# Five forms of the product that reads the middle rows of a two-layer decoder trunk

## The chip, the cores and the metric

The kernel runs on one core of a Trainium2 chip. The metric is the device time of one execution in microseconds (us), as the median over several executions; lower is better. One execution was also recorded by the hardware profiler, and all rows shown below come from such recordings.

## The reference

Two layers over a sequence of 256 tokens with 2048 features, all in float32. Layer 0 mixes tokens by retention with 8 heads, layer 1 by a short gated convolution of width 3. Each mixer is followed by a SwiGLU feed-forward block with 5632 inner features. Each sub-layer is fed by an RMS norm with a scale and shift that come from the conditioning vector `c`, and is added back with a gate.

```python
for i in range(DEPTH):
    mod = (c_act @ w_mod[i] + b_mod[i])[:, None, :]
    sh1, sc1, g1, sh2, sc2, g2 = jnp.split(mod, 6, axis=-1)
    h = (rms_norm(x, norm1_g[i]) * (1.0 + sc1) + sh1).astype(x.dtype)
    ...          # i = 0: y = retention_mixer(h, ...); i = 1: y = short_conv_mixer(h, ...)
    x = (x + g1 * y).astype(x.dtype)
    h = (rms_norm(x, norm2_g[i]) * (1.0 + sc2) + sh2).astype(x.dtype)
    x = (x + g2 * swiglu(h, ffn_w_in[i], ffn_w_out[i])).astype(x.dtype)
return rms_norm(x, final_g).astype(x.dtype)

def swiglu(h, w_in, w_out):
    a, b = jnp.split(h @ w_in, 2, axis=-1)
    return (jax.nn.silu(a) * b) @ w_out
```

## The kernel before

Features lie on the 128 partitions and the 256 tokens along the free dimension, so an activation of 2048 features is 16 rows of 128x256. Every float32 value is kept as a sum of two parts, a high one and a low one. A row therefore holds 2 x 256 numbers: the 256 tokens' high parts and then their low parts. A weight block of 128x128 is split in the same way into `hi` and `lo`. A product of a block with a row needs three partial products: `hi` with the row's high part, `hi` with its low part, and `lo` with its high part.

`product` (line 345) makes them with two matmuls for each block: `hi` against all 512 numbers of the row (line 355), which fills both halves of a PSUM bank, and `lo` against the 256 high parts (line 358), added to the second half. I call these two matmuls a *unit*. `packed` (line 365) makes the same three partial products with three matmuls of 256 columns (lines 378 to 380) that are all added into one half of a bank. It is used for the queries, keys and gates of the retention, and for the last column of an output. `values` (line 794) holds the activation as the stationary operand and streams 512 columns of weights in each of its three matmuls (lines 801 to 803).

A `Group` is a list of output columns (128 features each) and of rows `ks`. `product` walks over the rows and, for each row, over the columns. Weights come in one long stream in just this order of use: `laid_out` writes them so, `prepare` (line 295) takes 1 MB from memory, and for each half of it (8 units) ScalarE makes the `hi` part (line 310) and VectorE the `lo` part (line 313). `take` keeps two such halves prepared ahead. TensorE's instructions are issued in the order of the program text. The order on the other engines is chosen by the compiler's scheduler from priorities.

Five stages read *middle rows*, the tiles `mid`:

| stage | what | rows | units with 512 columns | packed units |
|---|---|---|---|---|
| 0 | layer 0, feed-forward, first half of the inner features | 22 | 352 | 0 |
| 1 | layer 0, feed-forward, second half | 22 | 330 | 22 |
| 2 | layer 1, output of the convolution | 16 | 240 | 16 |
| 3 | layer 1, feed-forward, first half | 22 | 352 | 0 |
| 4 | layer 1, feed-forward, second half | 22 | 330 | 22 |

Each is an `output` (line 517) over 16 columns. Its first group takes two columns together (four in stage 2) and all but the last two rows (the last one in stage 2), so that the stage can begin before the last middle rows are written. Then each of these columns gets its remaining rows, and the other columns follow one at a time. After a column, two VectorE instructions add it to the residual `x[j]` (lines 535 and 536). In the second half of a feed-forward block, and in stage 2, squares for the next norm follow, and `scaled_only` (line 461) writes the next stage's row `h[j]`. The last column of those stages is `packed`. Between the columns `paced` (line 267) lets through the modulation steps (line 244), each of them 1 MB from memory and one VectorE instruction over 128x2048.

Before the change each middle row is a tile of its own, 22 tiles of 2 KB on each partition. The rows `h` that the other stages read are slices of one tile, `h_all`, in which one row is 2 x 258 numbers long (line 458).

Of the kernel before, what the change touches and what calls it, by code (L numbers as in the profile page):

```python
# [49 lines left out]
RAW_BUFS = 3  # L50
PART_BUFS = 4
# [49 lines left out]

def halves(rows):
    n = rows // P // 2
    return [range(n), range(n, 2 * n)]
# [25 lines left out]
FFN_OUT = out_groups(halves(DFF), 2, LEAD_FFN)  # L130


def in_use_order():
# [10 lines left out]
    for layer in range(DEPTH):  # L144
        if layer == 1:
            for g in CONV_IN:
                yield "conv_w_in", 0, g
            for g in CONV_OUT:
                yield "conv_w_out", 0, g
        for part in range(2):  # L150
            for g in FFN_IN[part]:
                yield "ffn_w_in", layer, g
            for g in FFN_OUT[part]:
                yield "ffn_w_out", layer, g
# [31 lines left out]
def trunk(ctx: ExitStack, tc: tile.TileContext, x_in, c_in, pos_in, w_mod, cols_in, tab_in, w_all, out):  # L186
# [158 lines left out]
    def product(g, act, base=0, before=None, banks=None, last=True):  # L345

        fresh = not banks
        banks = banks or [bank() for _ in g.cols]
        for k in g.ks:
            if before:  # L350
                before(k)
            h = act[k - base]
            for c, pt in zip(g.cols, banks):
                hi, lo = take(g, k, c)
                nc.tensor.matmul(  # L355
                    pt, hi, h, start=fresh and k == g.ks[0], stop=False, skip_group_check=True
                )
                nc.tensor.matmul(  # L358
                    pt[:, 1, :], lo, h[:, 0, :], start=False, stop=last and k == g.ks[-1], skip_group_check=True
                )  # L360
            ticked(len(g.cols))
        paced(len(g.cols) * len(g.ks))
        return banks
# [153 lines left out]
    def output(groups, act, which, last, after=None, base=None):  # L517
# [5 lines left out]
        for j, g in enumerate(groups):  # L523
# [9 lines left out]
            (pt,) = product(g, act, base, banks=banks[j : j + 1])  # L533
# [378 lines left out]
    mpool = ctx.enter_context(tc.tile_pool(name="mpool", bufs=1))  # L912

# [4 lines left out]
    def swiglu(layer, acc, after):  # L918
        n = FT // 2
        for part, groups in enumerate(FFN_IN):  # L920
            mid = [mpool.tile([P, 2, S], F32R, tag=f"mid{i}", name=name("mid")) for i in range(n)]
# [14 lines left out]
            acc = output(FFN_OUT[part], mid, (layer, GT2), part == 1, after if part else None)  # L936
# [5 lines left out]
    mid = [mpool.tile([P, 2, S], F32R, tag=f"mid{i}", name=name("mid")) for i in range(KT)]  # L942
# [82 lines left out]
```

## Time and profile before

| | us |
|---|---|
| median of three runs | 2654.03 |
| lowest, highest run | 2652.48, 2657.95 |
| span of the profiled execution | 2658.0 |

The span, from the first to the last instruction of the profiled execution, is as long as the highest of the runs, so there is nothing to add around it. It is 4.0 us (0.15%) above the median.

How to read the rows: PE is TensorE with its matmuls, PEld are its weight loads, which overlap the matmuls. DVE is VectorE, ACT is ScalarE, SP the queue that issues loads. In a row of a group of instructions stand line, engine, operation, output and inputs, shapes, count, busy time, mean nanoseconds of one, and then the idle time of the engine before them with what ended it. The duration of a matmul has a modelled end and overlaps the next one. What counts is the distance from one start to the next.

### The profile page before, as it was taken

The page shows a single profiled execution, that of the slowest core. Times are in us where ns is not written, and L with a number is a line of the kernel's source. Part 1 is how long each engine was busy: PE and PEld are TensorE (multiplying, and loading weights), DVE is VectorE, ACT ScalarE, POOL GpSimd, SP SyncE. Part 2 cuts the span into 40 slices and gives each one's busy share as a digit, 9 for nine tenths or more (in the row PEclk, how much of TensorE's full clock was granted, in tenths as well). Part 3 has the DMA queues.
Part 4 walks back from the last instruction along what each step waited for, and adds up shares of the span by engine and source line. Part 5 has one row for each costly group of instructions (what it writes and reads, how often), then busy time and mean ns, then how long its engine had stood idle before and what let it go on. Part 6 is the DMA issues. An engine that isn't in the chain of part 4 may idle for free.

```text
span 2658.0 us, 40105 instructions
## 1 busy us (share of the span) xinstructions
PE 2622.0 (99%) x16044; PEld 2340.2 (88%) x16044; DVE 2019.7 (76%) x2646; ACT 1260.0 (47%) x1819; POOL 153.5 (6%) x230
## 2 busy tenths in 40 slices
PE   7999999999999999999999999999999999999998
PEld 6998889889989888888888898888998888888887
DVE  7888988787698877777777889878887665555554
ACT  5545543444456444344444454444554443444443
POOL 0000000120000010100000001100000000000000
PEclk9999999999999999999999999999999999999999
DMA  9975668777676876777777758776776755444453
GB/s 397 396 274 220 224 232 315 263 269 280 239 271 252 319 282 262 300 269 280 283 278 276 273 219 321 289 276 258 265 269 256 264 220 190 184 187 189 190 190 127
DMA packets 96958, 687.70 MB, mean 259 GB/s; under 512 B 10753, under 2 KB 12545, under 8 KB 13825
## 3 DMA queue, kind: packets, MB, share of 16 engines
q1 hardware_dynamic: 96194, 684.48, 67.6%
q8 instruction: 125, 2.05, 0.3%
q10 hardware_dynamic: 576, 0.66, 0.1%
q14 instruction: 63, 0.52, 0.1%
HBM read 682.99 MB, written 2.10 MB: 258 GB/s over the span
## 4 chain that ended last, share of the span: by engine, by line
PE 75%; issue 19%; DVE 3%; DMA 1%; ACT 0%; POOL 0%; SPq 0%; POOLq 0%; ACTq 0%; DVEq 0%
PE bank L355 35%; PE bank L358 18%; PE bank L380 4%; PE bank L378 4%; PE bank L379 4%; PE bank L802 2%; PE bank L803 2%; PE bank L801 2%; PE bank L494 1%; PE bank L493 1%; PE bank L495 1%; DMA raw<-w_all 1%; DMA raw<-w_mod 1%; DVE lo L313 1%; DVE raw L619 0%
## 5 line engine op out<-in xcount | busy, mean ns | idle before, releaser
L313 DVE TENSOR_TENSOR lo<-raw,hi 128x1024 fp32r<-128x1024 f32 x912 | 1112.6, 1224 | 550.1 <-ACT hi L310 548.1
L310 ACT CAST hi<-raw 128x1024 fp32r<-128x1024 f32 x912 | 953.6, 1050 | 1101.8 <-PE bank L355 632.4
L355 PE MATMUL bank<-h,hi 128*128 128x512 f32 x3296 | 1155.2, 395 | 0.0
L358 PE MATMUL bank<-h,lo 128*128 128x256 f32 x3296 | 926.2, 281 | 0.0
L355 PEld LDWEIGHTS bank<-h,hi 128*128 128x128 f32 x3296 | 623.0, 189 | 144.1
L358 PEld LDWEIGHTS bank<-h,lo 128*128 128x128 f32 x3296 | 623.3, 189 | 0.0
L355 PE MATMUL bank<-mid,hi 128*128 128x512 f32 x1604 | 557.4, 394 | 0.0
L358 PE MATMUL bank<-mid,lo 128*128 128x256 f32 x1604 | 446.0, 278 | 0.0
L244 DVE SCALAR_TENSOR_TENSOR raw<-raw,cb 128x2048 f32<-128x2048 f32 x160 | 365.7, 2286 | 12.5 <-DMA raw<-w_mod 12.0
L355 PEld LDWEIGHTS bank<-mid,hi 128*128 128x128 f32 x1604 | 301.2, 188 | 70.2
L358 PEld LDWEIGHTS bank<-mid,lo 128*128 128x128 f32 x1604 | 301.5, 188 | 0.0
L380 PE MATMUL bank<-h,lo 128*128 128x256 f32 x1024 | 292.0, 285 | 6.2 <-DVE lo L313 6.2
L378 PE MATMUL bank<-h,hi 128*128 128x256 f32 x1024 | 291.9, 285 | 3.5 <-ACT h L644 3.5
L379 PE MATMUL bank<-h,hi 128*128 128x256 f32 x1024 | 291.3, 284 | 0.0
L380 PEld LDWEIGHTS bank<-h,lo 128*128 128x128 f32 x1024 | 195.7, 191 | 7.1 <-DVE lo L313 7.1
L378 PEld LDWEIGHTS bank<-h,hi 128*128 128x128 f32 x1024 | 197.3, 193 | 3.9 <-ACT h L644 3.8
L379 PEld LDWEIGHTS bank<-h,hi 128*128 128x128 f32 x1024 | 195.9, 191 | 0.2 <-DVE h L645 0.2
L355 PE MATMUL bank<-rm,hi 128*128 128x512 f32 x496 | 175.9, 399 | 0.1
L358 PE MATMUL bank<-rm,lo 128*128 128x256 f32 x496 | 139.5, 281 | 0.0
L355 PEld LDWEIGHTS bank<-rm,hi 128*128 128x128 f32 x496 | 93.3, 188 | 22.7 <-DVE rm L395 0.4
L802 PE MATMUL bank<-lo,h 128*128 128x512 f32 x256 | 101.8, 398 | 4.2 <-DVE lo L313 4.2
L801 PE MATMUL bank<-hi,h 128*128 128x512 f32 x256 | 102.2, 399 | 0.0
(155 smaller groups left out, 2190.2 us busy)
## 6 DMA issues: line engine op xcount, KB each, us to landing
raw<-w_all SPq DMA_DIRECT2D x456, 1024.0 KB, 4.9
raw<-w_mod SPq DMA_DIRECT2D x192, 1024.0 KB, 5.1
x<-x_in SPq DMA_DIRECT2D x4, 512.0 KB, 5.7
decay<-tab_in SPq DMA_DIRECT2D x8, 128.0 KB, 3.7
out<-out SPq DMA_DIRECT2D x4, 256.0 KB, 3.1
out<-out ACTq DMA_DIRECT2D x3, 128.0 KB, 2.7
out<-out SPq DMA_DIRECT2D x1, 384.0 KB, 2.6
out<-out ACTq DMA_DIRECT2D x1, 256.0 KB, 3.2
```

Source lines behind the costliest of these rows:

```text
L244: nc.vector.scalar_tensor_tensor(raw, raw, 1.0, cb, op0=ALU.mult, op1=ALU.mult, accum_out=total)
L310: nc.scalar.copy(hi, raw)
L313: nc.vector.tensor_tensor(lo, raw, hi.bitcast(F32), op=ALU.subtract)
L355: nc.tensor.matmul(pt, hi, h, start=fresh and k == g.ks[0], stop=False, skip_group_check=True)
L358: nc.tensor.matmul(pt[:, 1, :], lo, h[:, 0, :], start=False, stop=last and k == g.ks[-1], skip_group_check=True)
L378: nc.tensor.matmul(pt, hi, h[:, 0, :], start=first, stop=False, skip_group_check=True)
L379: nc.tensor.matmul(pt, hi, h[:, 1, :], start=False, stop=False, skip_group_check=True)
L380: nc.tensor.matmul(pt, lo, h[:, 0, :], start=False, stop=last, skip_group_check=True)
L493: nc.tensor.matmul(pt, hi, rows[0], start=k == 0, stop=False)
L801: nc.tensor.matmul(o, ht[:, 0, :], hi, start=k == 0, stop=False)
L802: nc.tensor.matmul(o, ht[:, 0, :], lo, start=False, stop=False)
L803: nc.tensor.matmul(o, ht[:, 1, :], hi, start=False, stop=k == KT - 1)
```

## The change

All middle rows move into one tile, `mid_all`. `MID_AT` gives each stage the place of its rows in it, and `FORMS` names a form for each stage:

- Stage 0: a row starts every 516 numbers instead of every 512, thus 16 bytes later on each further row.
- Stage 1: the single columns from the third to the fourteenth are put into groups of two (`in_twos`). In any group of exactly two columns, the order for a row becomes `hi` of the first, `hi` of the second, `lo` of the first, `lo` of the second. The first groups of stages 0, 1, 3 and 4 have two columns as well, and so take this order too.
- Stage 2: `FORMS` has the entry "runs" for it, with run lengths in `CONV_RUNS`. The call of `output` for this stage (line 963 before) is not part of the diff and passes no form.
- Stage 3: `hi` is applied to the row's high and low part in two matmuls of 256 columns, so that a unit has three matmuls of 256 columns.
- Stage 4: even rows lie every 512 numbers from the start, odd rows every 512 numbers from `EVEN` on, which is 11 rows and 128 numbers further.

```diff
+FORMS = (None, "two", "runs", "three", None)
+CONV_RUNS = (4, 8, 16, 32)
+ROW = 2 * S
+EVEN, N_MID = ROW * (DFF // P // 4) + S // 2, DFF // P // 2
+MID_SIZE = EVEN + N_MID // 2 * ROW
+MID_AT = [[i * ROW for i in range(N_MID)] for _ in range(5)]
+MID_AT[0] = [i * (ROW + 4) for i in range(N_MID)]
+MID_AT[4] = [i // 2 * ROW + i % 2 * EVEN for i in range(N_MID)]
...
+def in_twos(groups, lead):
+
+    first, ends, rest = groups[0], groups[1 : 1 + lead], groups[1 + lead : -1]
+    last = groups[-1]
+    twos = [Group(a.cols + b.cols, ks=a.ks) for a, b in zip(rest[::2], rest[1::2])]
+    odd = rest[len(twos) * 2 :]
+    return [first] + ends + twos + odd + [last]
...
-FFN_OUT = out_groups(halves(DFF), 2, LEAD_FFN)
+FFN_OUT = [out_groups(halves(DFF), 2, LEAD_FFN) for _ in range(DEPTH)]
+FFN_OUT[0][1] = in_twos(FFN_OUT[0][1], LEAD_FFN)
...
-    def product(g, act, base=0, before=None, banks=None, last=True):
+    def product(g, act, base=0, before=None, banks=None, last=True, form=None):
...
+            held_back = []
             for c, pt in zip(g.cols, banks):
                 hi, lo = take(g, k, c)
-                nc.tensor.matmul(
-                    pt, hi, h, start=fresh and k == g.ks[0], stop=False, skip_group_check=True
-                )
-                nc.tensor.matmul(
-                    pt[:, 1, :], lo, h[:, 0, :], start=False, stop=last and k == g.ks[-1], skip_group_check=True
-                )
+                to, of = pt, h
+                if isinstance(form, int):
+                    to, of = [t.rearrange("p a (n r) -> p n a r", r=form) for t in (pt, h)]
+                start = fresh and k == g.ks[0]
+                if form == "three":
+                    for i in range(2):
+                        nc.tensor.matmul(
+                            pt[:, i, :], hi, h[:, i, :], start=start and not i, stop=False, skip_group_check=True
+                        )
+                else:
+                    nc.tensor.matmul(to, hi, of, start=start, stop=False, skip_group_check=True)
...
+                if len(g.cols) == 2:
+                    held_back.append(low)
+                else:
+                    low()
+            for low in held_back:
+                low()
...
-        for j, g in enumerate(groups):
+        made = iter([])
+        for g, j in [(g, c // P) for g in groups for c in g.cols]:
             needed(*which, j)
...
-            (pt,) = product(g, act, base, banks=banks[j : j + 1])
+            pt = next(made, None)
+            if pt is None:
+                runs = CONV_RUNS[j % len(CONV_RUNS)] if form == "runs" else form
+                made = iter(product(g, act, base, banks=banks[j : j + 1], form=runs))
+                pt = next(made)
...
+    mid_all = mpool.tile([P, MID_SIZE], F32R, tag="mid", name="mid")
+
+    def mid_rows(stage):
+        return [
+            mid_all[:, at : at + 2 * S].rearrange("p (a b) -> p a b", a=2) for at in MID_AT[stage]
+        ]
...
-            mid = [mpool.tile([P, 2, S], F32R, tag=f"mid{i}", name=name("mid")) for i in range(n)]
+            mid = mid_rows(3 * layer + part)
...
-            acc = output(FFN_OUT[part], mid, (layer, GT2), part == 1, after if part else None)
+            acc = output(
+                FFN_OUT[layer][part], mid, (layer, GT2), part == 1, after if part else None, form=FORMS[3 * layer + part]
+            )
...
-    mid = [mpool.tile([P, 2, S], F32R, tag=f"mid{i}", name=name("mid")) for i in range(KT)]
+    mid = mid_rows(2)
```

`low` in the diff is a function that issues the matmul of `lo` as before.

More of the change, by code (lines that the diff above doesn't have):

```diff
@@ L152, in in_use_order @@
                 yield "ffn_w_in", layer, g
[L153 removed]
+            for g in FFN_OUT[layer][part]:
                 yield "ffn_w_out", layer, g
@@ L515, in normed, with output @@
         return [lambda dst=None, pt=pt: total(pt, dst) for pt in banks]
-    def output(groups, act, which, last, after=None, base=None):
+    def output(groups, act, which, last, after=None, base=None, form=None):
         layer, gate = which[0], mod_g[which[0]][which[1] == GT2]
```

5 lines of the change are left out of this document (added).

## The prediction

> **What bounds the kernel now.** I read the page first: the span, the busy shares and the granted clock, then the chain, then the groups of the matmuls that read `mid`.
>
> ```profile
> span 2658.0 us, 40105 instructions
> PE 2622.0 (99%) x16044; PEld 2340.2 (88%) x16044; DVE 2019.7 (76%) x2646; ACT 1260.0 (47%) x1819; POOL 153.5 (6%) x230
> ...
> PEclk9999999999999999999999999999999999999999
> ...
> PE 75%; issue 19%; DVE 3%; DMA 1%; ACT 0%; POOL 0%; SPq 0%; POOLq 0%; ACTq 0%; DVEq 0%
> ...
> L355 PE MATMUL bank<-mid,hi 128*128 128x512 f32 x1604 | 557.4, 394 | 0.0
> L358 PE MATMUL bank<-mid,lo 128*128 128x256 f32 x1604 | 446.0, 278 | 0.0
> ```
>
> TensorE is busy 99% of the span, at nine tenths or more of its clock in every slice, and it carries the chain ("issue" is time that the chain can't explain). The matmuls that the change touches never wait: 0.0 us of idle time before them. So the time of the five stages is the number of their matmuls by the distance between starts. The means of 394 and 278 ns are no prices, since matmuls overlap. Their busy times here add up to 1003 us, and the next view shows that the units take less than that.
>
> So I cut windows from the first `hi` product of a stage to the next kind of product. The view was asked for line 358, of which each unit has one. The PEld count is the number of units; PE counts one matmul more, which reaches in over the edge.
>
> ```profile
> core 0: us, PE busy (x) PEld busy (x), PEclk, DMA share, GB/s
> 1052.31:1174.33 122.02, 97.73 (x353) 66.13 (x352) 1.00 0.72 275
> 1174.34:1421.03 246.69, 197.84 (x705) 133.18 (x704) 1.00 0.74 282
> 1421.04:1535.43 114.39, 91.61 (x331) 62.00 (x330) 1.00 0.71 269
> 1814.85:1842.23 27.38, 21.93 (x80) 14.85 (x79) 1.00 0.64 242
> 1842.24:1899.11 56.87, 45.29 (x162) 30.47 (x161) 1.00 0.77 290
> 2153.96:2275.98 122.02, 97.73 (x353) 66.13 (x352) 1.00 0.51 189
> 2522.68:2637.08 114.40, 91.62 (x331) 61.96 (x330) 1.00 0.44 169
> ```
>
> In stages 0, 1, 3 and 4 (first, third and the last two rows) a unit takes 122.02/352 = 346.6 ns, in each of them. The second row is the input product of the feed-forward block, which reads `h`: 246.69/704 = 350.4 ns. Stage 2 has both: 79 units at 346.6 ns, and then 161 at 56.87/161 = 353.2 ns, with the same code, rows and places. So a unit has at least two rhythms, 6.6 ns apart, and neither the granted clock (1.00 in all rows) nor a waiting matmul separates them.
>
> What stands at the border of the two, at 1842 us:
>
> ```profile
> 1833.81 2.29 DVE L244 SCALAR_TENSOR_TENSOR raw<-raw,cb 128x2048 f32<-128x2048 f32 x1
> ...
> 1836.20 0.88 DVE L535 SCALAR_TENSOR_TENSOR sum<-bank,g,x 128x256 f32<-128x256 f32 x2
> ...
> 1841.36 1.22 DVE L313 TENSOR_TENSOR lo<-raw,hi 128x1024 fp32r<-128x1024 f32 x1
> ...
> 1842.59 0.40 PE L355 MATMUL bank<-mid,hi 128*128 128x512 f32 x1
> 1842.64 0.19 PEld L358 LDWEIGHTS bank<-mid,lo 128*128 128x128 f32 x1
> ```
>
> VectorE spent from 1833.81 to 1841.36 on a modulation step and the sums of the four columns that ended together, then made the next `lo` weights, and one weight load came 0.05 us behind its `hi` matmul. No time to speak of was lost in that wait, but the rhythm changed for the rest of the stage.
>
> **Part by part.** The sum is made against the profiled span; the forecast adds it to the median, which lies 4.0 us below the span, for I know of nothing in the five stages that would scale with that difference.
>
> *Stage 3, three matmuls.* As a first half it has no packed column, so all its 352 units get one more matmul and one more weight load. The nearest row is the packed column of stage 1, which has this form on the same kind of row (asked for line 380, one per unit):
>
> ```profile
> 1535.44:1543.34 7.90, 6.06 (x22) 4.22 (x22) 1.00 0.84 332
> ```
>
> A unit of three takes 7.90/22 = 359.1 ns, or 119.7 ns for each matmul, and 359.1 - 346.6 = 12.5 ns more than a unit of two. That makes 352 x 12.5 = +4.4 us, all of it on the path, since no matmul here waits for anything that could cover it. The difference to the packed form is that the three matmuls write both halves of the bank instead of one; the unit of two does so as well. Its bounds are 0 if splitting were free (a rival below), and +4.6 us if it costs as much as the two rhythms lie apart twice (2 x 6.6 ns).
>
> *Stage 1, two columns at a time.* The same matmuls in another order: `hi hi lo lo`, where 512 columns follow 512 and 256 follow 256. For 512 after 512 I take the stream of `values`, eight distances from the first to the last of these rows:
>
> ```profile
> 538.85 0.39 PE L801 MATMUL bank<-hi,h 128*128 128x512 f32 x1
> ...
> 540.71 0.39 PE L803 MATMUL bank<-hi,h 128*128 128x512 f32 x1
> ```
>
> 1.86 us/8 = 232.5 ns. A unit now is then 232.5 + 114.1. In the new order a 256 that follows a 256 has the 119.7 ns of the packed row, and the one ahead of the next 512 keeps 114.1: 2 x 232.5 + 119.7 + 114.1 = 698.8 for two units, 349.4 each, +2.8 ns. The first group (40 units) and six pairs (12 x 22) make 304 units: +0.9 us. Upper end: both at 119.7, +5.6 ns, +1.7 us. Lower end: nothing forbids that the new order falls into a better rhythm; I put that as far below as the slow one lies above, -6.6 ns, -2.0 us.
>
> The pairs also end two columns at once. What VectorE then does, and how far ahead the weights are, shows in the groups of stage 1 (1421 to 1543 us), for VectorE
>
> ```profile
> L244 DVE SCALAR_TENSOR_TENSOR raw<-raw,cb 128x2048 f32<-128x2048 f32 x10 | 22.9, 2289 | 3.0 <-DMA raw<-w_mod 3.0
> L536 DVE SCALAR_TENSOR_TENSOR x<-bank,g,sum 128x256 f32<-128x256 f32 x15 | 7.2, 482 | 0.3
> L466 DVE SCALAR_TENSOR_TENSOR h<-x,a,h 128x256 fp32r<-128x256 f32 x15 | 7.2, 481 | 0.0
> L535 DVE SCALAR_TENSOR_TENSOR sum<-bank,g,x 128x256 f32<-128x256 f32 x15 | 7.2, 480 | 1.8 <-PE bank L358 1.8
> L405 DVE TENSOR_TENSOR acc<-acc,sq 128x256 f32<-128x256 f32 x14 | 5.9, 419 | 0.0
> ```
>
> and for ScalarE, in the same stretch:
>
> ```profile
> L310 ACT CAST hi<-raw 128x1024 fp32r<-128x1024 f32 x44 | 46.3, 1052 | 62.3 <-PE bank L355 49.8 <-ACT h L465 4.9 <-DMA raw<-w_all 2.1
> ```
>
> A column's end costs 0.480 + 0.482 + 0.419 + 0.481 = 1.86 us of VectorE, two of them 3.7. ScalarE's wait is mostly for TensorE to give back a weight buffer (49.8 of 62.3 us): the preparation is ahead, held back by the use. The two halves ahead last 16 x 0.3466 = 5.5 us, and cover 3.7. At 1842 us the ends of four columns and a modulation step cost 0.05 us. I count 0; without the cover it is a rival below. `paced` is now called once for 44 units instead of twice for 22 with the same allowance in sum, so two modulation steps may follow each other on the queue that also issues the weights; the same number of them is due, and I count 0 here too.
>
> *The first groups of stages 0 and 4* take the same new order in 40 units each: 80 x 2.8 ns = +0.2 us (bounds -0.5 and +0.4).
>
> *Stage 0, rows of 516 numbers.* Rows of `h` start 516 numbers apart as well, and there a unit has 350.4 ns: 352 x 3.8 = +1.3 us. That is the nearest row but not the same, since the second half of an `h` row also starts 258 numbers, not 256, after the first. The bounds are a rhythm as far below 346.6 ns as the slow one is above, and the slow one, 2.3 us to either side. The Trainium skill says ("Advanced Engine Details and Errata", section "SBUF Cachelines") that SBUF lines have 16 bytes and that an operand is slowed where successive accesses fall on different lines; a shift by whole lines would then cost nothing, and the sum below would be 1.3 us less. No run here shows which of the two offsets of `h` makes its 3.8 ns.
>
> *Stage 4, odd rows elsewhere.* A row is as long as before and starts elsewhere by a multiple of 128 numbers. In stage 2 the rhythm changed without any change of place. I take 0, with 330 x 6.6 = 2.2 us to either side.
>
> *Stage 2.* The entry "runs" reaches nothing: `FORMS` is read at 3 x layer + part, which is 0, 1, 3 or 4, and the call of the convolution passes no form. It keeps 240 units of 512 columns. If its late weight load is gone, the rhythm stays at 346.6: 161 x 6.6 = -1.1 us. The sums of the four columns are still there, so I take 0.
>
> *One tile for all rows.* A product could now wait for the last write into the tile instead of for its own row. For `h_all`, also one tile, this shows that it doesn't:
>
> ```profile
> 1543.35 0.28 PE L493 MATMUL bank<-h,hi 128*128 128x258 f32 x1
> ...
> 1545.71 0.48 DVE L466 SCALAR_TENSOR_TENSOR h<-x,a,h 128x256 fp32r<-128x256 f32 x1
> ```
>
> The first product reads `h_all` while its last row is still written, 2.4 us later. So 0.
>
> The sum: 4.4 + 0.9 + 0.2 + 1.3 = +6.8 us, 2654.0 + 6.8 = 2660.8 us. A measurement of this kernel tells about 0.2%, 5.3 us, from no change, so the sum lies just beyond that.
>
> **The rivals.** *The split is free.* If two matmuls of 256 columns took just the time of one of 512 (2 x 116.3 ns), stage 3 would cost 0: +2.4 us, 2656.4. Against it stands the packed row, 119.7 ns for each matmul, with the first `hi` loaded twice there too; for it only that a 256 ahead of a 512 takes 114.1. The Trainium skill ("TensorE: Matmul & The Clock Gate", section "Back-to-back issue gap") gives columns/2.4 + 2.5 ns for a distance at full clock, so that an extra matmul costs 2.5 ns, 0.9 us in stage 3, and the sum would be 3.3; the 232.5 and 119.7 ns here are 17 and 10 ns above that formula. Chance 0.06.
>
> *A better rhythm, faster than before.* The place of a row or the order could set the rhythm, and the old one need not be the best. It decides at the unit: stages 0, 1 and 4 (352, 304 and 330 units) have to win more than the 4.4 us of stage 3, so 4.5 ns in each unit. With two steps of 6.6 ns they win 986 x 13.2 = 13.0 us, and the sum is 4.4 - 13.0 = -8.6 us, 2645.4. For it: the two rhythms of stage 2. Against it: four stages and the faster part of stage 2 all have 346.6, and the differing places of `h` made units slower. Chance 0.05.
>
> *Weights come late in stage 1.* With a modulation step a pair's end takes 3.7 + 2.3 us, and the next `lo` is 1.2 us later, 7.2 us in all, against 5.5 us of weights ahead: 1.7 us for each of six pairs, 10 us, 2670.8 us. Against it: the same heap at 1842 us cost 0.05 us. It decides once VectorE is away from L313 for over 5.5 us. Chance 0.07.
>
> *The one tile serializes.* The last middle row of a stage is written well after its first product:
>
> ```profile
> 1052.31 0.39 PE L355 MATMUL bank<-mid,hi 128*128 128x512 f32 x1
> ...
> 1057.44 0.42 DVE L395 TENSOR_TENSOR mid<-m,mid 128x256 fp32r<-128x256 f32 x1
> ```
>
> A wait for it would cost 5.6 us in each of five stages, 28 us, 2688.8. Chance 0.03.
>
> **How the numbers follow.** My forecast keeps 0.79. Within it the rhythms of stages 0, 1, 2 and 4 move the sum by about 2 us to either side, so two thirds of it (0.54) lie beyond +5.3 us and 0.24 within it, with 0.01 below. Slower is 0.54 + 0.07 + 0.03 = 0.64, the same is 0.24 + 0.06 = 0.30, faster 0.06. The range goes from 2655, where the free split and the low rhythms are held, to 2668, which holds the upper ends (4.6 + 1.7 + 0.4 + 2.3 + 2.2 = 11.2 us, 2665.2) and part of the late weights; it leaves out the faster case, the serial one and the edges, under 0.2.
>
> **What would show it.** TensorE should have 16044 + 352 = 16396 matmuls, with `mid,hi` of 512 columns still 240 times in stage 2. Stage 3 should last 126.4 us instead of 122.0, at 359 ns a unit; if it keeps 122, the split is free. Stage 0 should show 350 ns, stage 1 349, stage 4 347; 353 in one of them means the slow rhythm, and below 343 in any of them the third rival. Idle time before matmuls of `mid`, released by L313's successor or by the writes of the middle rows, would show the last two rivals. The prediction is wrong if stage 3 gains under 3 us, or if the other four together move by over 4.

## The result and the profile after

The changed kernel takes 2664.36 us (median of 11 runs), the kernel before 2657.15 (11 runs). The ratio is 1.0029, with a 95% interval of 1.0021 to 1.0037: slower by 0.29%, where +0.26% (+6.8 us) was forecast; the two medians lie 7.2 us apart. The forecast time, 2660.8 us, stood on a median of three runs; with eleven runs that median is 3.1 us higher. The page of the profile after:

```profile
span 2663.0 us, 40726 instructions
PE 2627.3 (99%) x16356; PEld 2356.3 (88%) x16356; DVE 2017.7 (76%) x2646; ACT 1259.0 (47%) x1819; POOL 154.7 (6%) x230
```

TensorE still sets the time, now with 312 matmuls more. The next view has the same windows as before for the five stages, without their packed columns. It is asked for line 387, the product with `lo`, which each unit still has once. The columns are the window, its length, busy time and count of the matmuls, the same for the weight loads, the granted clock, and the share and rate of the DMA engines. The count of the weight loads is the number of units.

```profile
1050.03:1173.56 123.53, 95.43 (x353) 66.19 (x352) 1.00 0.72 273
1420.25:1535.34 115.09, 67.04 (x331) 62.02 (x330) 1.00 0.71 265
1814.77:1897.97 83.20, 66.48 (x241) 45.03 (x240) 1.00 0.73 272
2152.80:2279.04 126.24, 96.15 (x353) 67.42 (x352) 1.00 0.51 186
2525.75:2642.15 116.40, 89.32 (x331) 62.30 (x330) 1.00 0.45 166
```

Against the windows before (122.02, 114.39, 27.38 + 56.87, 122.02 and 114.40 us) this is, stage by stage:

| stage | form | forecast, us | measured, us |
|---|---|---|---|
| 0 | rows 16 bytes further each | +1.4 | +1.5 |
| 1 | two columns at a time | +0.9 | +0.7 |
| 2 | none (the entry is not used) | 0 | -1.1 |
| 3 | three matmuls | +4.4 | +4.2 |
| 4 | odd rows elsewhere | +0.1 | +2.0 |
| sum | | +6.8 | +7.4 |

The medians differ by 7.2 us, the two profiled spans by only 5.0: the first middle-row product started at 1052.31 us before and starts at 1050.03 now, so what lies ahead of it, which the change does not touch, was 2.3 us shorter in this execution, and 7.4 - 2.3 = 5.1. For 1.2 us of that the second output of the retention is responsible: its 180 units and packed column took 69.79 us before and 68.56 now, the slow rhythm and the fast one, with the same code. Such a flip can come with any one execution, so the agreement of 7.4 with the 7.2 us of the medians is no better than a microsecond or two. A recorded time is also longer than its span (2664.77 against 2663.0 us for the execution above), so the execution profiled before, with its span of 2658.0 us, was some 2659.8 us long, by estimate, and not the highest of the first three runs.

Where the 312 matmuls are, the groups of stage 3 show (line, engine, operation, shapes and count, then busy time, mean of one and idle time before):

```profile
L380 PE MATMUL bank<-mid,hi 128*128 128x256 f32 x624 | 112.4, 283 | 0.0
L387 PE MATMUL bank<-mid,lo 128*128 128x256 f32 x352 | 96.2, 282 | 0.0
L384 PE MATMUL bank<-mid,hi 128*128 128x512 f32 x40 | 12.5, 395 | 0.0
```

40 of the 352 units still have a `hi` product of 512 columns: `output` calls `product` for the first group without the form. No matmul waits, so everything that changed is distance between starts.

In stage 4 the single columns alone (the 286 units from the third column to the last but one):

```profile
2541.09:2642.14 101.05, 80.32 (x287) 54.03 (x286) 1.00 0.45 166
```

101.05/286 = 353.3 ns a unit, as long as a unit of the slow rhythm that stage 2 showed before. Stage 2 now has 83.20/240 = 346.7 throughout. So two things were open: what put stage 4 into the slow rhythm, the place of its rows or something else; and why a third matmul costs what it does.

### The profile page after: what moved, and what is told of

The parts are those of the page before. It is cut to its first block, busy times and chain, and to the rows that moved or that the text cites. A ratio compares the mean times of both kernels' runs of the same rounds, so it can differ in the third digit from the quotient of the medians.

```text
span 2663.0 us, 40726 instructions
## 1 busy us (share of the span) xinstructions
PE 2627.3 (99%) x16356; PEld 2356.3 (88%) x16356; DVE 2017.7 (76%) x2646; ACT 1259.0 (47%) x1819; POOL 154.7 (6%) x230
## 4 chain that ended last, share of the span: by engine, by line
PE 74%; issue 20%; DVE 3%; DMA 2%; ACT 1%; POOL 1%; POOLq 0%; SPq 0%; ACTq 0%; DVEq 0%
PE bank L384 34%; PE bank L387 17%; PE bank L416 4%; PE bank L414 4%; PE bank L415 4%; PE bank L843 2%; PE bank L844 2%; PE bank L842 2%; DMA raw<-w_all 1%; PE bank L530 1%; PE bank L529 1%; PE bank L531 1%; DVE lo L331 1%; DVE raw L262 1%; DMA raw<-w_mod 0%
## 5 line engine op out<-in xcount | busy, mean ns | idle before, releaser
L384 PE MATMUL bank<-mid,hi 128*128 128x512 f32 x1292 | 437.7, 396 | 0.0
L387 PE MATMUL bank<-mid,lo 128*128 128x256 f32 x1604 | 414.4, 280 | 0.0
L384 PEld LDWEIGHTS bank<-mid,hi 128*128 128x128 f32 x1292 | 227.5, 188 | 39.3
L380 PE MATMUL bank<-mid,hi 128*128 128x256 f32 x624 | 112.4, 283 | 0.0
```

Source lines behind the costliest of these rows:

```text
L380: nc.tensor.matmul(pt[:, i, :], hi, h[:, i, :], start=start and not i, stop=False, skip_group_check=True)
L384: nc.tensor.matmul(to, hi, of, start=start, stop=False, skip_group_check=True)
L387: nc.tensor.matmul(pt[:, 1, :], lo, h[:, 0, :], start=False, stop=last and k == g.ks[-1], skip_group_check=True)
```

## The experiments

The windows of experiments 1 to 7 are those of the single columns of stages 0, 1, 3 and 4 (308, 286, 308 and 286 units), with stage 2 (176 units) where it is shown; each is asked for the line of the `lo` product. These seven kernels keep the one tile of the changed kernel. The cuts of the edits leave lines out where "..." stands.

**1. Only the order of the first groups.**

```diff
-FORMS = (None, "two", "runs", "three", None)
+FORMS = (None,) * 5
-MID_AT[0] = [i * (ROW + 4) for i in range(N_MID)]
-MID_AT[4] = [i // 2 * ROW + i % 2 * EVEN for i in range(N_MID)]
-FFN_OUT[0][1] = in_twos(FFN_OUT[0][1], LEAD_FFN)
```

> The changed kernel with all forms and places undone (rows every 512 numbers, no pairs, no split), so that only two things are left: the one tile, and the order hi hi lo lo in the first groups of two columns. Stage 4 of the changed kernel ran 310 of its units at 353.1 ns. Theory A (the rhythm is handed over: the first group's order leaves the stream in the slow rhythm, and the single columns keep it): stages 0, 1, 3 and 4 show about 353 ns in their single columns, about 124.2 us for a stage instead of 122.0 or 122.3. Rival B (the place of the odd rows made it): all four stages show 346.6 ns in their single columns, and only the 40 units of the first group differ. Rival C (chance of an execution): some stages at 346.6, some at 353. Prediction's term for the first group: 349.4 ns a unit over 40 units.

```profile
1064.38:1173.20 108.82, 86.49 (x309) 58.18 (x308) 1.00 0.74 276
1435.25:1536.30 101.05, 80.32 (x287) 54.03 (x286) 1.00 0.73 269
2170.52:2279.34 108.82, 86.49 (x309) 58.18 (x308) 1.00 0.53 189
2541.40:2642.45 101.05, 80.32 (x287) 54.03 (x286) 1.00 0.46 166
```

353.3 ns in all four stages, with all rows at their old places and the old order in just these columns. Stage 4's 2.0 us come from the 40 units ahead of them, whose order was changed in passing. The place of the odd rows is not needed for it, and four times out of four is not chance. The whole kernel took 2665.14 us against 2656.83, in one run each.

**2. Only the places of the rows.**

```diff
-FORMS = (None, "two", "runs", "three", None)
+FORMS = (None,) * 5
...
+MID_AT[1] = [i * (ROW + 8) for i in range(N_MID)]
+MID_AT[2] = [i * (ROW + 32) for i in range(KT)]
+MID_AT[3] = [i * (ROW + 16) for i in range(N_MID)]
...
-FFN_OUT[0][1] = in_twos(FFN_OUT[0][1], LEAD_FFN)
...
-                if len(g.cols) == 2:
+                if False:
```

> The old order and the old forms everywhere, only the places of the rows differ: stage 0 a row every 516 numbers (16 bytes further on each row, as in the changed kernel), stage 1 every 520 (32 bytes), stage 2 every 544 (128 bytes), stage 3 every 528 (64 bytes), stage 4 the odd rows of the changed kernel (a multiple of 128 numbers away). Theory A (a shift within 64 bytes makes the unit dearer, a shift by whole 64 bytes does not, and stage 4's slow rhythm came from the order): stage 0 at 350 to 351 ns, stage 1 at 348 to 351, stages 2, 3 and 4 at 346.6. Rival B (place alone makes the slow rhythm): stage 4 at 353. Rival C (lines of 16 bytes, a shift by whole lines costs nothing): stages 0 to 4 all at 346.6, and the 350.9 ns of stage 0 came from the order of its first group.

```profile
1070.22:1178.38 108.16, 86.36 (x309) 57.94 (x308) 1.00 0.75 278
1440.46:1540.63 100.17, 80.05 (x287) 53.81 (x286) 1.00 0.74 272
1842.43:1903.72 61.29, 49.44 (x177) 33.20 (x176) 1.00 0.82 291
2173.91:2281.25 107.34, 86.31 (x309) 57.84 (x308) 1.00 0.54 191
2543.22:2642.36 99.14, 79.22 (x287) 53.70 (x286) 1.00 0.47 169
```

A shift of 16 bytes from row to row gives 351.2 ns, 32 bytes 350.2, 128 bytes (stage 2) 348.2, 64 bytes 348.5, and stage 4's odd rows 346.6. So stage 0's price is the place, stage 4's is not. Theory A is right for stages 0, 1 and 4 and wrong for 64 and 128 bytes, which it had as free; C, lines of 16 bytes, is wrong for all four shifts.

The packed columns, three matmuls of 256 to a unit, go the other way. Stage 1's 22 units on rows 32 bytes out of step (asked for the line of the packed `lo` product):

```profile
1540.64:1548.45 7.81, 6.01 (x22) 4.15 (x22) 1.00 0.86 308
```

7.81/22 = 355.0 ns, where rows in step had 359.1. So a shift is dear for 512 and 256 columns by turns and saved 4 ns here where only matmuls of 256 follow each other.

**3. The product of `hi` in pieces.** Rows in step and the old order; `form` is a tuple of widths:

```diff
+                    for n in form:
+                        nc.tensor.matmul(
+                            all_to[:, i : i + n], hi, all_of[:, i : i + n], start=start and not i, ...
+                        )
+                        i += n
...
-FORMS = (None, "two", "runs", "three", None)
+FORMS = ((256, 256), (384, 128), None, (128,) * 4, (128, 128, 256))
```

> Rows every 512 numbers and the old order. In the single columns the product of hi with the 512 numbers of a row is cut into pieces, lo stays one product of 256: stage 0 256+256, stage 1 384+128, stage 3 128+128+128+128, stage 4 128+128+256; stage 2 is as before. From the 232.5 ns of a 512 after a 512 and the 119.7 ns of a 256 after a 256, 256 columns are worth 112.8 ns and a matmul has 6.9 ns on top. Theory A (columns plus a fixed cost for each matmul): a 128 takes 63.3 ns and a 384 176.1, so a unit takes 359 ns in stage 0, 359 in stage 1, 373 in stage 3 and 366 in stage 4. Rival B (each matmul also needs its own weight load, which can not be faster than about 115 to 120 ns, so that no distance is under that): 359 ns in stage 0, about 411 to 416 in stage 1, 575 to 600 in stage 3, 460 to 479 in stage 4.

```profile
1064.71:1175.58 110.87, 87.15 (x309) 59.14 (x308) 1.00 0.74 273
1437.78:1554.08 116.30, 95.05 (x287) 53.63 (x286) 1.00 0.63 235
2188.80:2362.64 173.84, 102.30 (x309) 59.14 (x308) 1.00 0.34 120
2625.05:2757.56 132.51, 80.87 (x287) 54.91 (x286) 1.00 0.35 126
```

360.0, 406.6, 564.4 and 463.3 ns. Four pieces of 128 and a 256 take 564.4/5 = 112.9 ns each, so 128 columns cost as much as 256 nearly do. Theory A (373 ns) is out; B is right in kind, and its floor of 115 to 120 ns was a little high. The floor lies between weight loads, not between matmuls, as a unit of 384, 128 and 256 columns in stage 1 shows (start, duration):

```profile
1500.18 0.22 PE L378 MATMUL bank<-mid,hi 128*128 128x128 f32 x1
1500.18 0.19 PEld L386 LDWEIGHTS bank<-mid,lo 128*128 128x128 f32 x1
1500.24 0.33 PE L386 MATMUL bank<-mid,lo 128*128 128x256 f32 x1
1500.29 0.31 PEld L378 LDWEIGHTS bank<-mid,hi 128*128 128x128 f32 x2
```

The `lo` matmul starts 0.06 us after the one of 128 columns, but the next load only 0.11 us after the load before it. In stage 3 of this kernel the matmuls start 55 to 174 ns apart, the loads 108 to 124 ns apart, 112.9 on average. So each matmul there costs one such distance on average, with 128 columns or with 256. Halving a 512 costs little (13.4 ns), since a 256 takes 120 ns anyway, little more than that distance. In stage 1 three loads have 406.6 ns, more than three distances, so the floor alone does not give that time.

**4. The runs that were not used.** Old places, order and groups; the form now reaches the convolution:

```diff
...
-    acc = output(CONV_OUT, mid, (1, GT1), True, lambda j: scaled_only(1, 1, j))
+    acc = output(CONV_OUT, mid, (1, GT1), True, lambda j: scaled_only(1, 1, j), form=FORMS[2])
-FORMS = (None, "two", "runs", "three", None)
+FORMS = (2, 8, "runs", 64, 128)
```

> Rows every 512 numbers and the old order. The form of alternating runs is handed to the convolution's output, which the change had left without it: the single columns take runs of 4, 8, 16 and 32 numbers of the high and the low part by turns, in the row that is read and in the bank that is written; in the other stages the single columns take one run length each: 2 in stage 0, 8 in stage 1, 64 in stage 3, 128 in stage 4. The same sums come out. Theory A (only the number of columns and the rhythm count, the jumps in between are free): every stage at 346 to 354 ns a unit. Rival B (every jump costs): a unit grows as the runs get shorter, most of all at runs of 2 (8 bytes) in stage 0, where it would be over 400 ns, and by half as much with each doubling. Rival C (lines of 16 bytes): runs of 4 and more cost nothing, runs of 2 do.

```profile
1070.25:1209.86 139.61, 89.00 (x309) 57.83 (x308) 1.00 0.60 221
1471.88:1574.83 102.95, 80.75 (x287) 54.13 (x286) 1.00 0.71 265
1876.51:1939.75 63.24, 49.69 (x177) 33.30 (x176) 1.00 0.78 284
2209.83:2316.60 106.77, 85.32 (x309) 57.79 (x308) 1.00 0.54 192
2578.56:2677.69 99.13, 79.21 (x287) 53.66 (x286) 1.00 0.47 169
```

Runs of 2 numbers take 453.3 ns a unit, runs of 8 360.0, the mixture of 4 to 32 in stage 2 359.3 on average, runs of 64 and 128 346.7 and 346.6. Of runs of one number there is no time. In the mixture a column of runs of 16, and then one of runs of 32, show:

```profile
1888.03:1893.79 5.76, 4.53 (x17) 3.01 (x16) 1.00 0.80 269
1893.79:1899.44 5.65, 4.48 (x17) 3.07 (x16) 1.00 0.88 312
```

That is 360.0 and 353.1 ns a unit; runs of 4 have 360 as well. So there are steps, of about 7 ns at 32 numbers and 13 ns from 16 down to 4, and a steep price at 2 numbers, 8 bytes. Theory A is out, and rival C is nearest, though runs of 4 and more are not free. The Trainium skill ("Advanced Engine Details and Errata", sections "SBUF Cachelines" and "PSUM Cachelines") has lines of 16 bytes in SBUF, and wants every two consecutive elements contiguous in PSUM, where any non-contiguous pattern is said to slow matmuls significantly. The steep price at 8 bytes agrees with the lines of 16; runs of 2 meet the rule of two elements and are the dearest all the same; runs of 64 and 128 are not contiguous either and cost nothing here. Row and bank were stepped alike, so the two memories are not separated. Had the change reached stage 2 as its list says, it would have cost (63.24 - 61.00) = 2.2 us more there than the 346.6 ns that it kept.

**5. The halves of a row.**

```diff
...
+LAYOUT = ((11, 5760, 2818), (1, 544, 272), (1, 768, 384), (1, 528, 264), (11, 5760, 2816))
...
+            mid_all[:, i // n * row : i // n * row + 2 * half].rearrange("p (a b) -> p a b", a=2)[
+                :, :, i % n * S : i % n * S + S
+            ]
+            for n, row, half in [LAYOUT[stage]] for i in range(KT if stage == 2 else N_MID)
```

> Old order and old forms; only the distance between the two halves of a row and between rows differ. So far: rows shifted against each other by 16, 32, 64 and 128 bytes had 351.2, 350.3, 348.5 and 348.3 ns a unit, rows at multiples of 512 bytes 346.6, and the rows of h (16 bytes, halves 8 bytes off) 350.4. Here: stage 0 rows 1024 bytes apart with the halves 8 bytes off a multiple of 512 bytes; stage 1 halves 272 and rows 544 numbers apart (64 and 128 bytes off); stage 2 halves 384 and rows 768 apart (no offset within 512 bytes); stage 3 halves 264 and rows 528 apart (32 and 64 bytes off); stage 4 rows 1024 bytes and halves 11264 bytes apart (no offset). Theory A (what counts is where a read begins within 512 bytes against where the one before ended; halves count as rows do): stages 2 and 4 at 346.6, stage 0 at 350 to 352, stages 1 and 3 at 348 to 350. Rival B (only the start of the row counts, the second half does not): stages 0, 2 and 4 at 346.6, stage 1 at 348.3, stage 3 at 348.5.

```profile
1069.89:1178.71 108.82, 87.02 (x309) 59.14 (x308) 1.00 0.74 276
1440.75:1540.84 100.09, 80.58 (x287) 53.91 (x286) 1.00 0.74 272
2174.83:2282.90 108.07, 86.61 (x309) 58.17 (x308) 1.00 0.53 190
2544.86:2644.00 99.14, 79.22 (x287) 53.70 (x286) 1.00 0.47 169
```

353.3, 350.0, 350.9 and 346.6 ns. Halves that lie far apart, but without an offset within 512 bytes, cost nothing (stage 4); halves 8 bytes off cost 6.7 ns although the rows are in place (stage 0). That stage is as long as in the slow rhythm, but it is another stream: in the trace its products start 234 and 119 ns apart in every unit, while in the slow rhythm of experiment 1 three units take turns, with 232, 241 and 235 ns after the `hi` product. So halves count as rows do: B is out, A right in kind and 1 to 2 ns off in stages 0 and 3. Stage 2 had a late weight load in its second single column and ran at 346.6 before it and 353.3 after it.

**6. A nudge between first group and single columns.** The first experiment's kernel, with units of three in the tail groups:

```diff
+NUDGED = ((0, 1), (0,), (), (1,), (0, 1))
...
+        order_new[0] = stage != 4
+                runs = "three" if j in NUDGED[stage] else None
```

> The kernel with only the new order of the first groups, where all four feed-forward stages ran their single columns at 353.3 ns, and between the first group and the single columns some units of three matmuls: all four units of the tail groups in stage 0, the first two in stage 1, the last two in stage 3. Stage 4 has the old order in its first group and four units of three behind it. Theory A (the rhythm is a state of the stream that is handed on, and each of the two lasts until something disturbs it): at least one of stages 0, 1 and 3 goes back to 346.6 ns for all its single columns, about 6 us less than 353.3 over 308 units gives 2.0 us, and stage 4 may fall to 353.3. Rival B (the order of the first group decides by the places of weights and banks that it leaves, not by timing): stages 0, 1 and 3 keep 353.3 and stage 4 keeps 346.6.

```profile
2538.44:2639.48 101.04, 80.32 (x287) 54.03 (x286) 1.00 0.46 166
```

This is stage 4, at 353.3 ns; stages 0, 1 and 3 have the times of experiment 1 again within 0.01 us, so 353.3 everywhere. Units of three did not heal stages 0, 1 and 3, against theory A's first half, and they put stage 4 into the slow rhythm although its first group had the old order, against rival B.

**7. Other orders.** `product` takes its order as a word, here by stage for first group, two tail groups and single columns:

```diff
+FORMS = (("llhh", "hl", "hl", "hl"), ("hl", "lh", "lh", "lh"), None, ("hhll", "hl", "lh", "hl"), ("hl", "hl", "lh", "hl"))
...
```

> Rows every 512 numbers, no splits, no pairs; only the order of the same two matmuls differs by stage. So far the slow rhythm (353.3 ns) came whenever the single columns were entered from two or more matmuls of 256 columns in a row (the order hi hi lo lo, or units of three), and the fast one (346.6) when they were entered from units of hi and lo. Stage 0: the first group goes lo lo hi hi, so that the single columns are entered from 512 after 512. Stage 1: first group as before, but all later units go lo, hi instead of hi, lo; the change of order puts one 256 behind a 256 once. Stage 3: first group hi hi lo lo as in the changed kernel, but the last tail group of two units goes lo, hi, so that the single columns are entered from a 512 behind a 512. Stage 4: first group as before and the same last tail group lo, hi. Theory A (256 after 256 leaves the slow rhythm, 512 after 512 the fast one): single columns at 346.6 in stages 0, 3 and 4, 353.3 in stage 1. Rival B (any break of the old alternation leaves the slow one): all four at 353.3. Rival C (the order hi, lo itself is the cause of both rhythms): stage 1 at another time than either.

```profile
1064.45:1171.22 106.77, 86.24 (x309) 58.21 (x308) 1.00 0.75 281
1432.95:1532.09 99.14, 80.07 (x287) 54.05 (x286) 1.00 0.74 275
2166.03:2275.07 109.04, 86.50 (x309) 58.18 (x308) 1.00 0.53 189
2536.81:2636.19 99.38, 80.08 (x287) 54.05 (x286) 1.00 0.47 169
```

346.6 in stages 0 and 1, 353.3 in stage 3 and 346.6 in stage 4 (the last two windows begin 0.23 us early, with the last `hi` product of the tail group, which is left out of these two figures). All three rules fall: A in stages 1 and 3, B in stages 0, 1 and 4, C in stage 1. What the pair of stages 3 and 4 shows is worth more: their last four units before the single columns are the same, and still each keeps the rhythm that its first group left. The rhythm behaves as a state of the stream, handed on through units of either order. But stage 4 was fast again behind the slow stage 3: the state did not outlast the 704 units of `h`, whose rows are out of step.

**8. Rows of `h` in place.** The kernel before, with halves at multiples of 512 bytes for the largest reader:

```diff
-PART_BUFS = 4
+PART_BUFS = 3
...
-    h_all = hpool.tile([P, KT, 2, S + 2], F32R, tag="h", name="h")
-    h = [h_all[:, j, :, :S] for j in range(KT)]
+    h_flat = hpool.tile([P, KT * 640 + 128], F32R, tag="h", name="h")
+    h = [h_flat[:, j * 640 : j * 640 + 768].rearrange("p (a b) -> p a b", a=2)[:, :, :S] for j in range(KT)]
...
```

> The kernel before with the rows of h laid out so that every half begins at a multiple of 512 bytes (halves 384 and rows 640 numbers apart instead of 258 and 516); the two extra columns of a norm's first group hold the high and the low part of the shift, one behind the other, and are added afterwards. To make room, the prepared weights have three buffers instead of four. Theory A (places within 512 bytes decide, for h as for the middle rows): the 704 units of the second half's input go from 350.4 to 346.6 ns, 2.7 us less, or to 353.3 if they are entered in the slow rhythm, 2.0 us more; the stages of middle rows stay as in the kernel before. Rival B (h has 350.4 for another reason): 350.4 as before. What three buffers cost in the retention, where weights come late already, is not known from any run: between 0 and some 10 us.

The 704 units of the second half's input in layer 0 and in layer 1, and then the stages 0 and 3 ahead of them:

```profile
1189.26:1437.99 248.73, 197.71 (x705) 132.98 (x704) 1.00 0.75 277
2293.28:2537.32 244.04, 197.11 (x705) 133.06 (x704) 1.00 0.53 190
1064.88:1189.25 124.37, 98.85 (x353) 66.49 (x352) 1.00 0.74 271
2171.25:2293.27 122.02, 98.55 (x353) 66.53 (x352) 1.00 0.54 193
```

`h` takes 353.3 ns a unit in layer 0 and 346.6 in layer 1, not 350.4: theory A, which allowed both. Stage 0, ahead of the slow `h`, is slow itself, and stage 3 fast; the `h` units ahead of stage 0 had become slow too, at 353 ns in the trace. The kernel as a whole is slower, 2674.36 us against 2657.79, in one run each. Matmuls of `h` and of the middle rows that had 0.0 us of idle time now wait for `lo` weights:

```profile
L358 PE MATMUL bank<-h,lo 128*128 128x256 f32 x3296 | 924.5, 280 | 2.2 <-DVE lo L313 2.2
L358 PE MATMUL bank<-mid,lo 128*128 128x256 f32 x1604 | 449.9, 280 | 1.4 <-DVE lo L313 1.4
```

The idle time ahead of all matmuls adds up to 39.5 us in the trace, 26.6 before, which is 13 of the 14.6 us between the two spans (2672.6 and 2658.0). That points at the three weight buffers and not at the rows, but three buffers with the old rows were not run.

**9. Orders in the retention's and the convolution's outputs.** The kernel before, with an order for each output's first group and later units:

```diff
+ORDERS = {"ret0": ("lh all", "hl"), "ret1": ("lh all", "hl"), "conv": ("lh all", "hl"), "ffn": ("hl", "hl")}   # lows first
+ORDERS = {"ret0": ("lh", "lh"), "ret1": ("hl all", "hl"), "conv": ("hl all", "hl"), "ffn": ("hl", "hl")}   # other orders
...
```

> The kernel before, and only the order in the first groups of the retention's two outputs (six columns) and of the convolution's output (four columns) changed: for each row first all lo products, then all hi products; everything else in the old order. In the kernel before, both outputs of the retention, which follow on matmuls of 256 columns, run at 353.8 ns a unit (the second after a wait sometimes at 346.6), the convolution's starts at 346.6. Theory A (a first group that ends on 512 after 512 hands over the fast rhythm, as in stage 0 of the last experiment): the first output's 196 units go from 69.34 to about 68.0 us, the second's from 69.8 to about 68.4, the convolution's stays at 346.6 until a late weight load. Rival B (the first group's order can only break a rhythm, not set one; what comes before it decides): 69.3 and 69.8 stay, and the convolution may fall to 353.3.

> As the experiment before, with other orders: in the first output of the retention every unit goes lo, hi instead of hi, lo; in the second output and in the convolution's the first group has for each row all hi and then all lo products. Theory A (hi hi ... lo lo leaves the slow rhythm, for six and four columns as for two; lo, hi alone changes nothing): first output 69.3 us, second 69.8, the convolution's single columns at 353.3 from the start, about 90.2 us. Rival B (only the entry of exactly two columns did that): the convolution's single columns begin at 346.6.

The two outputs of the retention in the kernel before, then with the lows first, then with the other orders, where the convolution's units from the fifth column on are the last row:

```profile
373.98:443.31 69.33, 54.98 (x196) 37.10 (x196) 1.00 0.75 283
733.44:803.23 69.79, 50.65 (x180) 34.07 (x180) 1.00 0.73 275
```

```profile
374.71:444.14 69.43, 68.08 (x196) 36.70 (x196) 1.00 0.77 284
731.05:799.85 68.80, 61.68 (x180) 33.58 (x180) 1.00 0.76 278
```

```profile
372.41:440.45 68.04, 67.83 (x196) 36.66 (x196) 1.00 0.77 286
728.13:797.50 69.37, 62.57 (x180) 33.66 (x180) 1.00 0.74 272
1829.90:1898.30 68.40, 62.45 (x180) 33.66 (x180) 1.00 0.76 276
```

Lows first left the first output slow, against A. Lo, hi throughout made it fast (68.04/196 = 347.1 ns), which the A of that run did not have. The convolution, after a first group of four `hi` and four `lo`, was fast (its window holds two `lo` products of the first group, 0.24 us, then 180 units at 346.7 and a packed column of 16 at 360 ns), again against A, so the rule of two columns does not carry over to four. The second output tells nothing about orders: in experiments 1 to 7, which leave the retention as it was, it ran slow in 1, 2 and 4 and fast in 3, 5, 6 and 7. The first output was slow in all seven.

**10 and 11. The other order in more places.** `lo`, `hi` in the mixers' outputs alone, and everywhere in `product`:

```diff
+ORDERS = {"ret0": ("lh", "lh"), "ret1": ("lh", "lh"), "conv": ("lh", "lh"), "ffn": ("hl", "hl")}   # in the mixers
+ORDERS = {"ret0": ("lh", "lh"), "ret1": ("lh", "lh"), "conv": ("lh", "lh"), "ffn": ("lh", "lh")}   # and order="lh" by default
...
```

> The kernel before with one difference: in the two outputs of the retention and in the output of the convolution every unit goes lo, hi instead of hi, lo. The first output of the retention went from 69.34 to 68.05 us by this in the last experiment. Theory A (the rhythm of a stage is the same in both orders and is set at its start; lo, hi enters the fast one): both outputs of the retention near 68.1 and 68.4 us, the convolution's between 89 and 90, in sum 2.5 to 3.5 us less than before, a ratio of 0.9987 to 0.9990. Rival B (chance of one execution): 69.3 and 69.8 as before, ratio 1.000.

> As the experiment beside it, and also all single columns of the feed-forward blocks and of the convolution's input, those that read h included, go lo, hi. Theory A (the places of the rows set the time of a unit of h, not the order): h stays at 350.4 ns, the middle rows at 346.6, and the ratio is that of the experiment beside it. Rival B (the order changes what h costs): 704 units between 346.6 and 353.3, from 2.7 us less to 2.0 more in each of the four large stages of h.

In the mixers: 2654.20 us (11 runs) against 2657.72 (15 runs), ratio 0.9990 (0.9982 to 0.9999), just clear of 1. The first output of the retention is fast again, with the 68.04 us of the last experiment; the second, shown here, is not:

```profile
728.12:797.90 69.78, 63.71 (x180) 33.81 (x180) 1.00 0.72 274
```

So theory A's number came out without its mechanism: it counted on a gain in all three outputs. The first is 1.3 us shorter, in this run as in experiment 9 and in the kernel below, and that part of the 3.5 us is shown. The convolution stayed fast behind its late weights, but so it did with the old order in experiments 3 and 6; the rest of the gain is not explained.

Everywhere: 2669.43 us (5 runs), ratio 1.0047 (1.0033 to 1.0061). The middle rows stay at 346.7 (122.04 us for the 352 units of stage 0), but `h` pays:

```profile
1172.43:1421.74 249.31, 249.31 (x705) 133.63 (x704) 1.00 0.74 278
```

354.1 instead of 350.4 ns a unit, and 3296 units by 3.7 ns are 12.2 us, about the 11.7 us that the kernel lost. For rows with offsets the order counts too, as rival B had it.

## Why the prediction was right, point by point

**What bounds the kernel.** TensorE by the distance between starts: right. No matmul of the middle rows waits, and the stages' differences, with the 2.3 us ahead of them, add up to the difference of the two spans within 0.1 us.

**Stage 3.** The price of a unit was read from the packed column (359.1) and is 360.0. The count was off: 312 units, not 352, since the first group gets no form. That misreading of the code cost 0.5 us. The mechanism is shown by experiment 3: the same split in stage 0 has 360.0 ns again, where the free split would have 346.6. By the formula of the Trainium skill ("TensorE: Matmul & The Clock Gate", section "Back-to-back issue gap") four pieces of 128 would add, as an estimate, 4 x 55.8 - 215.8 = 7 ns; they add 218 here. The same section of the Trainium skill calls the formula that of an isolated matmul and says that it under-counts small ones that load their own weights, for which it has about 81 ns at 128 columns. The prediction left that limit out; 112.9 ns were measured here.

**Stage 1.** +2.8 ns a unit was forecast from two rows of other stages. It came to +0.7 us. The pairs ran at 348.4 ns, +1.8, and the one single column behind them at 353.4, in the slow rhythm: two small misses in opposite directions, so the sum is better than its terms. VectorE's double heap at a pair's end delayed nothing, as counted.

**Stage 0.** +3.8 ns from the rows of `h`, +4.6 measured. That it is the place, and not the order, experiment 2 shows. Lines of 16 bytes alone, by which the shift would have been free, do not describe these rows.

**Stage 4, the step that failed.** The forecast took 0 for the places, which was right, and 0.1 us for the first group, which was right too: the 44 units ahead of the single columns took 15.34 us, and 15.26 before. It missed that the first group hands its rhythm on: 286 units at 6.7 ns, 1.9 us. Its own bound of 2.2 us covers that, and 353 ns in a stage is the sign that it had named for the slow rhythm. The two rhythms had been seen in stage 2, and the flip there was laid to a wait; that an order could set it was only considered for the units in that order.

**Stage 2.** That the "runs" reach nothing was right. The late weight load did not come back in this execution, so 1.1 us went the other way. It hit stage 4's miss from the other side, and the total looks better than its terms: that part of the agreement is luck.

**The rivals.** Late weights and the one tile as a barrier: no matmul waits, so neither. The free split: out by 4.2 us in stage 3. A better rhythm than 346.6 was never seen for these units.

## What to carry to other kernels

When TensorE is back to back, price a new form by a row of the trace that already has that form (here the packed column), count the units by the code that really passes it, and mind that a matmul of up to 256 columns cost here about as much as the 113 ns between two weight loads. Try rows, and their halves, at multiples of 512 bytes if matmuls of 512 and 256 columns read them by turns: 3.8 ns on each of the 3296 units of `h` would be 12.5 us of this kernel, by estimate. No run here was faster by it, though: in experiment 8 the rows of `h` in place had 346.6 ns in one layer, but 353.3 in the other, which is more than the 350.4 they had out of place, and packed units were cheaper on rows out of step. And look at what follows a changed group, not only at the group: the same instructions ran at 346.6 or 353.3 ns for hundreds of units, depending on what came before.

## What the runs showed of the hardware that was not expected

- A stream of units (512 and 256 columns by turns) on rows without offsets has two steady speeds, 346.6 and 353.3 ns. In the trace the distances repeat after two units when it is fast, and after three when it is slow. It kept the one it was in through changes of stage, of weights and of rows where all rows were in step (experiment 8), but not across rows out of step (experiment 7). It can change at a late weight load (in stage 2 it was slow behind one in experiments 1, 5 and 7, fast in 3 and 6), at units of three matmuls, or at another order. Which entry leads to which speed was not found: three rules were tried in experiment 7 alone, and all fell.
- The start of a read counts: 16, 32, 64 and 128 bytes from row to row gave 351.2, 350.2, 348.5 and 348.2 ns, second halves 8 bytes off 353.3, and multiples of 512 bytes 346.6. A shift of 256 bytes was not run, and why the start counts is open.
- Weight loads started no less than 108 ns apart in experiment 3, and 112.9 on average where they follow each other closely, while matmuls of 128 columns started as little as 55 ns after each other.
